# A rotating start for the projection's weights in their SBUF tile

## The chip, the cores and the metric

The kernel runs on one core of a Trainium2 chip. A core has TensorE (matmuls; the profile calls it PE, and its loading of weights PEld), VectorE (DVE), ScalarE (ACT), GpSimd (POOL) and SyncE (SP), which issues most of the DMAs. The metric is the time of one execution on the device in microseconds. The median of 3 runs before the change is 859.98 us (859.38 to 860.38).

## The reference

One layer of a decoder, for one sequence of 512 tokens and a model width of 2048, all in float32:

```python
h = rmsnorm(x, norm_g[l])
proj = h @ w_in[l]
(cv_a, cv_b, cv_gate, fq, fk, fv, f_logit, fox_gate,
 mq, mem_gate) = jnp.split(proj, SPLITS, axis=-1)
...
y = jnp.concatenate([y_conv, y_fox, y_mem], axis=-1)
x = x + y @ w_out[l]
return rmsnorm(x, final_g)
```

Behind the input projection stand three groups: a causal depthwise convolution of 31 taps with layer norm (512 channels), a forgetting attention of 8 heads of 128, and a cross attention of 4 heads into 256 memory tokens. Each is gated by a SiLU of its own part of the projection. The change is in the input projection, h @ w_in, which the kernel computes 128 output features at a time.

## The kernel before

**Two parts for each operand.** A float32 operand of a matmul is split into a high and a low part of the type float32r: ACT copies the raw tile into the high part (L93), DVE subtracts the high part from the raw tile and writes the low one (L94). A product is then three matmuls, high x high, high x low and low x high, which are summed in PSUM (mm3, L104 to L106; product, L739).

**The weights' tiles.** weights (L134) loads 2048 x 128 of w_in in two halves of 8 rows of 128, each with one DMA into a raw tile of 128 x 1024 elements (pool of 6), and calls operand (L120) on each. operand takes a tile "wb" of 2 x 1024 + 128 elements per partition from a pool of 3. The high part starts at element off of the tile and the low part 1024 elements later; the 128 spare elements are the room that off may use. off is in elements of 4 bytes. Three values are in use: PAIRED = 0, EVEN = 8 (32 bytes) and HEADS = 16 (64 bytes). Within a part, row k of 128 elements starts at 512 k bytes.

**The two forms of the projection.** The normalised input lies in SBUF for the whole projection, transposed and split, as tiles hh0 to hh7 and hl0 to hl7, two rows of 512 tokens in each.

- project (L304) computes 128 features for all 512 tokens: 16 rows x 3 matmuls with the weights stationary and 512 columns moving, with off=EVEN. It is called 22 times: 8 times for the convolution's two inputs, 4 times each for the memory queries, the memory gates and the convolution's gates, and twice for the first head's queries and keys.
- pair (L717) computes two times 128 features for all tokens with seven products of half the size in place of eight (Strassen's scheme): the raw weights are added and subtracted on DVE (less, L710), the sums of the input's quarters stand ready in the tiles s0, s1, s2. Each of its seven products calls operand with off=0 and runs 8 rows x 3 matmuls with 256 columns moving (L739). There are 15 pairs.

The other users of wb tiles are the memory's keys (L275, EVEN), the memory's values (L232) and the convolution's pointwise product (L593), both at 0, the output's plain part (L942, EVEN; there wb is the moving operand) and the output's heads (L983, HEADS; wb is the moving operand too).

**Addresses.** The pools put each of the three wb tiles 448 bytes past a multiple of 512, and all the moving tiles of the projection (hh, hl and the sums) 480 bytes past one. So project's weights start at 480, like its moving operand, and a pair's weights at 448, 32 bytes short of it, in terms of the place within 512 bytes.

**Order.** Every engine runs its instructions in order; the kernel's framework fixes that order ahead and puts in the semaphores. The weights' DMAs stand on SP's queue. With three wb tiles, one is read by TensorE while another is filled, and a third stands ready or is being filled.

Of the kernel before, what the change touches and what calls it, by code (L numbers as in the profile page):

```python
# [17 lines left out]
P = 128  # L18
S = 512
D = 2048  # L20
KT = D // P
# [26 lines left out]
def hybrid_layer_kernel(  # L48
# [20 lines left out]
    w_in, w_mem_kv, w_out, w_pw = w_in[0], w_mem_kv[0], w_out[0], w_conv_pw[0]  # L69
# [10 lines left out]
    def nm(s):  # L80
        uid[0] += 1
        return f"{s}_{uid[0]}"

    def pj(shape=(P, S)):
        return ps_pj.tile(list(shape), F32, tag="pj", name=nm("pj"))
# [4 lines left out]
    def split(hi, lo, src, scale=None):  # L90

        if scale is None:
            ins = nc.scalar.copy(hi, src)  # L93
            nc.vector.tensor_tensor(lo, src, hi.bitcast(F32), ALU.subtract)  # L94
        else:
            ins = nc.scalar.activation(hi, src, AF.Identity, scale=scale)
            nc.vector.scalar_tensor_tensor(
                lo, src, scale, hi.bitcast(F32), ALU.mult, ALU.subtract
            )
        return ins.ins  # L100

    def mm3(o, a, b, start, stop):
        (ah, al), (bh, bl) = a, b
        nc.tensor.matmul(o, ah, bh, start=start, stop=False)  # L104
        nc.tensor.matmul(o, ah, bl, start=False, stop=False)  # L105
        nc.tensor.matmul(o, al, bh, start=False, stop=stop)  # L106
# [3 lines left out]
    def background(n):  # L110
        for _ in range(min(n, len(bg))):
            bg.popleft()()

    def raw_tile(n, c):
        return wp.tile([P, n, c], F32, tag="raw", name=nm("raw"), bufs=6)

    PIECE = 8 * P
    PAIRED, EVEN, HEADS = 0, 8, 16

    def operand(src, out=None, off=0):  # L120

        if out is None:
            both = wp.tile([P, 2 * PIECE + P], F32R, tag="wb", name=nm("wb"), bufs=3)
            out = tuple(
                both[:, o : o + PIECE].rearrange("p (n c) -> p n c", c=src.shape[2])
                for o in (off, off + PIECE)
            )  # L130
        split(*out, src)
        return out

    def weights(src, n, c, raw=None, off=0):  # L134

        half = n // 2
        src = src.rearrange("(k p) f -> p k f", p=P)
        parts = []
        for j in range(2):
            rows = slice(j * half, (j + 1) * half)  # L140
            r = raw_tile(half, c) if raw is None else raw[:, rows, :]
            nc.sync.dma_start(out=r, in_=src[:, rows, :])
            parts.append(operand(r, off=off))
        return lambda k: tuple(t[:, k % half, :] for t in parts[k // half])


# [27 lines left out]
    with tc.tile_pool(name="start", bufs=1) as st:  # L174
# [49 lines left out]
        for q in range(4):  # L224
            qs = slice(q * QC, (q + 1) * QC)
            for t in range(MT):
                nc.sync.dma_start(out=mrow[t][:, qs], in_=mem[t * P : (t + 1) * P, qs])
            raw = None
            if q >= 2:
                raw = st.tile([P, D], F32, tag="rows", name=f"rv{q}", bufs=4)  # L230
                raw = raw.rearrange("p (k f) -> p k f", f=MW)
            wvs.append(weights(w_mem_kv[q * QC : (q + 1) * QC, MW : 2 * MW], 4, MW, raw))  # L232
            if q == 0:
                small, cwr = load_small()
                pt = at((P, KT))
                nc.tensor.transpose(pt, mgain, ident[:KT, :KT])
                nc.vector.tensor_copy(cols[:, :KT], pt)
            for k in range(4 * q, 4 * q + 4):
                pt = at((P, M))
                for t in range(MT):  # L240
                    nc.tensor.transpose(
                        pt[:, t * P : (t + 1) * P], mrow[t][:, k * P : (k + 1) * P], ident
                    )
                last = split(m_hi[k], m_lo[k], pt, scale=cols[:, k : k + 1])
            for kk in range(4):
                k = 4 * q + kk
                for t in range(MT):
                    sl = slice(t * P, (t + 1) * P)
                    mm3(os_[t], (m_hi[k][:, sl], m_lo[k][:, sl]), wvs[q](kk), k == 0, k == KT - 1)
# [24 lines left out]
        for h in range(NM):  # L274
            wk = weights(w_mem_kv[:, h * P : (h + 1) * P], KT, P, off=EVEN)  # L275
            load_x(h)
            norm_x(h)
            o = pj((P, M))
            for k in range(KT):
                mm3(o, wk(k), (m_hi[k], m_lo[k]), k == 0, k == KT - 1)  # L280
                if h == NM - 1:
                    x_column(k)
            if h == 0:
                pt = at((P, M))
                for t in range(MT):
                    nc.tensor.matmul(
                        pt[:, t * P : (t + 1) * P], ones, diag[:, t, :], start=True, stop=True
                    )
                nc.vector.tensor_copy(rbc, pt)
            kt = st.tile([P, M], F32, tag="kt", name=nm("kt"), bufs=1)  # L290
            nc.vector.tensor_tensor(kt, o, rbc, ALU.mult)
            split(mk[0][:, h, :], mk[1][:, h, :], kt)
# [10 lines left out]

    def project(f0, per=0):  # L304

        w = weights(w_in[:, f0 : f0 + P], KT, P, off=EVEN)
        o = pj()
        for k in range(KT):
            mm3(o, w(k), (h_hi[k], h_lo[k]), k == 0, k == KT - 1)
        background(per)  # L310
        return o
# [11 lines left out]
    with tc.tile_pool(name="conv", bufs=1, reuse_waits="tile") as cp:  # L323
# [19 lines left out]
        def conv_in(c):  # L343
            oa = project(C_A + c * P, 6)
            ob = project(C_B + c * P, 6)
            up = cp.tile([P, PAD + S], F32, tag="up", name=nm("up"), bufs=3)
            nc.gpsimd.memset(up[:, 0:PAD], 0.0)
            sg = cp.tile([P, S], F32, tag="sgb", name=nm("sgb"), bufs=2)
            nc.scalar.activation(sg, ob, AF.Sigmoid)
            nc.vector.tensor_tensor(up[:, PAD:], oa, sg, ALU.mult)  # L350
            taps_of(c, up)
# [242 lines left out]
        for k in range(NC):  # L594
            wh, wl = wpw(k)
# [98 lines left out]
    with tc.tile_pool(name="fox", bufs=1, reuse_waits="tile") as fx:  # L694
# [11 lines left out]
        def plus(o, p, q):  # L706
            nc.vector.tensor_tensor(o, p, q, ALU.add)

        def less(o, p, q):
            nc.vector.tensor_tensor(o, p, q, ALU.subtract)  # L710

        def kept(src, tag):
            t = fx.tile([P, M], F32, tag=tag, name=nm(tag), bufs=1)
            nc.scalar.copy(t, src)
            return t

        def pair(fa, fb):  # L717

            HK = KT // 2

            def load(f0, half):
                r = raw_tile(HK, P)
                rows = slice(half * HK * P, (half + 1) * HK * P)
                nc.sync.dma_start(
                    out=r, in_=w_in[rows, f0 : f0 + P].rearrange("(k p) f -> p k f", p=P)
                )
                return r

            def product(o, w, a, start=False):
                wh, wl = operand(w)
                for k in range(HK):
                    ah, al = (t[:, k % 2, :] for t in a[k // 2])
                    for i, (p, q) in enumerate(((wh, ah), (wh, al), (wl, ah))):
                        nc.tensor.matmul(  # L739
                            o, p[:, k, :], q, start=start and k == 0 and i == 0,  # L740
                            stop=k == HK - 1 and i == 2, skip_group_check=True,
                        )

            b11, b12, b22, b21 = load(fa, 0), load(fb, 0), load(fb, 1), load(fa, 1)
            x1, zo, x2 = (pj((P, M)) for _ in range(3))
            product(x1, b11, a11, start=True)
            yield
            p1 = kept(x1, "p1")
            less(b11, b12, b11)
            product(zo, b11, s1, start=True)  # L750
            p5 = kept(zo, "p5")
            less(b11, b22, b11)
            product(x2, b11, s2, start=True)
            plus(x2, x2, p1)
            u2 = kept(x2, "u2")
            product(x1, b21, a12)
            product(zo, b22, s4)
            less(b12, b22, b12)
            product(x2, b12, s3)
            col = fx.tile([P, S], F32, tag="col", name=nm("col"), bufs=2)  # L760
            plus(col[:, M:], x2, p5)
            plus(col[:, :M], zo, u2)
            less(b21, b21, b11)
            yield
            product(x2, b21, a22)
            yield (x1, x2), col
# [320 lines left out]
```

## Time and profile before

| what | us |
|---|---|
| median of the runs | 859.98 |
| the profiled execution's own time | 860.89 |
| its span, first to last instruction | 859.0 |
| TensorE busy | 844.9 |
| DVE busy | 703.7 |
| ACT busy | 435.6 |

The span divides into stages, read in windows of the trace: up to about 75 us the memory's keys and values and the transposes of the input; from there to 343 us the 22 calls of project (two of them for the first head), with the convolution's taps on DVE and the memory attention between them; from 343 to about 677 us the 15 pairs with the forgetting attention between them; then the output projection. A row of a group in the profile gives line, engine, operation, operands and count, then the busy time, the mean length of one instruction and the idle time ahead of it. In the chain of work that ended last, a row gives the start, the length and what ran, with a count where equal pieces are merged.

### The profile page before, as it was taken

Reading aid. Unit: us, or ns where it says so; the run is one execution under the profiler, and the core shown is the slowest. Engines: PE = TensorE matmul, PEld = TensorE weight load, DVE = VectorE, ACT = ScalarE, POOL = GpSimd, SP = SyncE. Lnnn points to the kernel's source line nnn. Section 1 sums busy time; section 2 is a strip of 40 time slices with the busy share of each in tenths; the row PEclk is TensorE's granted clock in tenths of the full one; section 3 lists DMA queues with packets and bytes.
Section 4 is the critical chain, followed back from the end, with each engine's and each line's share of the span. In section 5 each row is a group of like instructions: output and inputs, shape, how many; then the busy total and the mean of one; then the engine's idle time right before and its main releaser. Section 6 shows DMA issues by size and latency. Waiting matters only on the chain.

```text
span 859.0 us, 14010 instructions
## 1 busy us (share of the span) xinstructions
PE 844.9 (98%) x5562; PEld 773.0 (90%) x5562; DVE 703.7 (82%) x1051; ACT 435.6 (51%) x679; POOL 46.6 (5%) x76
## 2 busy tenths in 40 slices
PE   8999999999999999999999999999999999999996
PEld 6898888888888888999999999999999888998995
DVE  4586799999987998988787879888887986876964
ACT  4874332224445544666565656556564942443523
POOL 1011000000000002010101010101010000000001
PEclk8999999999999999999999999999999999999999
DMA  9973234332432443333434343433334627361415
GB/s 312 336 214 80 74 96 111 98 98 75 109 86 82 115 110 99 93 108 96 123 99 123 94 109 94 111 103 100 106 81 157 229 78 265 98 197 50 148 49 195
DMA packets 143264, 107.51 MB, mean 125 GB/s; under 512 B 3892, under 2 KB 126816, under 8 KB 142560
## 3 DMA queue, kind: packets, MB, share of 16 engines
q1 hardware_dynamic: 141696, 102.52, 41.4%
q0 software_dynamic: 1504, 4.11, 1.4%
q8 instruction: 43, 0.70, 0.3%
q14 instruction: 21, 0.17, 0.1%
HBM read 98.46 MB, written 8.14 MB: 124 GB/s over the span
## 4 chain that ended last, share of the span: by engine, by line
PE 95%; ACT 2%; issue 1%; DVE 1%; DMA 1%; SPq 0%; POOL 0%; ACTq 0%; POOLq 0%
PE pj L739 33%; PE pj L104 13%; PE pj L105 13%; PE pj L106 13%; PE pj L988 8%; PE at L104 3%; PE at L105 3%; PE at L106 3%; PE at L827 1%; DMA raw<-in_w_mem_kv_dram 1%; ACT wb L93 0%; PE pj L415 0%; PE pj L416 0%; PE pj L269 0%; PE at L789 0%
## 5 line engine op out<-in xcount | busy, mean ns | idle before, releaser
L93 ACT CAST wb<-raw 128x1024 fp32r<-128x1024 f32 x205 | 215.4, 1052 | 246.1 <-PE pj L106 73.2
L94 DVE TENSOR_TENSOR wb<-raw,wb 128x1024 fp32r<-128x1024 f32 x205 | 250.0, 1221 | 64.2 <-ACT wb L93 60.3
L739 PE MATMUL pj<-hh,wb 128*128 128x256 f32 x960 | 177.3, 280 | 0.0
L739 PEld LDWEIGHTS pj<-hh,wb 128*128 128x128 f32 x960 | 150.1, 188 | 0.0
L104 PE MATMUL pj<-hh,wb 128*128 128x512 f32 x352 | 137.3, 391 | 0.1
L105 PE MATMUL pj<-hl,wb 128*128 128x512 f32 x352 | 137.4, 391 | 0.0
L106 PE MATMUL pj<-hh,wb 128*128 128x512 f32 x352 | 137.2, 390 | 0.0
L739 PE MATMUL pj<-hl,wb 128*128 128x256 f32 x480 | 134.2, 280 | 0.0
L710 DVE TENSOR_TENSOR raw<-raw,raw 128x1024 f32<-128x1024 f32 x76 | 92.7, 1219 | 1.3 <-DMA raw<-in_w_out_dram 0.8
L739 PEld LDWEIGHTS pj<-hl,wb 128*128 128x128 f32 x480 | 90.2, 188 | 0.0
L336 DVE SCALAR_TENSOR_TENSOR acc<-up,cwt,acc 128x512 f32<-128x512 f32 x120 | 85.0, 742 | 0.4
L988 PE MATMUL pj<-wb,rh 128*128 128x256 f32 x672 | 80.2, 280 | 0.7 <-DVE res L914 0.7
L988 PEld LDWEIGHTS pj<-wb,rh 128*128 128x128 f32 x672 | 79.5, 188 | 1.4 <-DVE res L914 1.1
L104 PEld LDWEIGHTS pj<-hh,wb 128*128 128x128 f32 x352 | 66.1, 188 | 14.0 <-PE pj L269 0.3
L106 PEld LDWEIGHTS pj<-hh,wb 128*128 128x128 f32 x352 | 66.1, 188 | 13.7
L105 PEld LDWEIGHTS pj<-hl,wb 128*128 128x128 f32 x352 | 66.1, 188 | 13.5
L739 PE MATMUL pj<-s0h,wb 128*128 128x256 f32 x240 | 48.1, 288 | 0.0
L739 PE MATMUL pj<-s1h,wb 128*128 128x256 f32 x240 | 45.7, 280 | 0.0
L739 PE MATMUL pj<-s2h,wb 128*128 128x256 f32 x240 | 44.8, 279 | 0.0
L739 PEld LDWEIGHTS pj<-s0h,wb 128*128 128x128 f32 x240 | 38.5, 188 | 0.0
L739 PEld LDWEIGHTS pj<-s1h,wb 128*128 128x128 f32 x240 | 38.1, 188 | 0.3
L739 PEld LDWEIGHTS pj<-s2h,wb 128*128 128x128 f32 x240 | 37.8, 188 | 0.0
(292 smaller groups left out, 1439.9 us busy)
## 6 DMA issues: line engine op xcount, KB each, us to landing
raw<-in_w_in_dram SPq DMA_DIRECT2D x104, 512.0 KB, 3.9
raw<-in_w_out_dram SPq DMA_DIRECT2D x32, 512.0 KB, 4.6
raw<-in_w_mem_kv_dram SPq DMA_DIRECT2D x12, 512.0 KB, 8.5
xr<-in_x_dram SPq DMA_DIRECT2D x4, 1024.0 KB, 8.5
res<-in_x_dram SPq DMA_DIRECT2D x8, 512.0 KB, 7.2
out_dram<-res SPq DMA_DIRECT2D x16, 256.0 KB, 2.9
rs<-yd SPq DMA_DIRECT2D x15, 256.0 KB, 4.5
mr<-in_mem_dram SPq DMA_DIRECT2D x8, 256.0 KB, 7.5
```

The lines of the kernel that those rows point to most:

```text
L93: ins = nc.scalar.copy(hi, src)
L94: nc.vector.tensor_tensor(lo, src, hi.bitcast(F32), ALU.subtract)
L104: nc.tensor.matmul(o, ah, bh, start=start, stop=False)
L105: nc.tensor.matmul(o, ah, bl, start=False, stop=False)
L106: nc.tensor.matmul(o, al, bh, start=False, stop=stop)
L336: return lambda: nc.vector.scalar_tensor_tensor(a, up[:, j : j + S], cwt[:, c, j : j + 1], a, ALU.mult, ALU.add)
L710: nc.vector.tensor_tensor(o, p, q, ALU.subtract)
L739: nc.tensor.matmul(o, p[:, k, :], q, start=start and k == 0 and i == 0, stop=k == HK - 1 and i == 2, skip_group_check=True,)
L827: nc.tensor.transpose(tp[:, (i - j) * P : (i - j + 1) * P], pr[i][:, j * P : (j + 1) * P], ident)
L988: nc.tensor.matmul(o[:, m, :], p, q[:, k, :], start=start and k + m + i == 0, stop=k == HK - 1 and i == 2, skip_group_check=True,)
```

## The change

A list of 23 offsets is made once, in elements: 0 to 15, then 16, 32, 48, 64, 80, 96 and 112, which is 0 to 60 bytes in steps of 4 and 64 to 448 bytes in steps of 64. It is walked round and round. Each half of project's weights takes the next offset of the list, and so does each of the seven products of a pair. All other users of wb tiles keep their offsets. The high and the low part still stand 1024 elements apart, so both move by the same offset.

```diff
@@ -116,6 +116,7 @@
     PIECE = 8 * P
     PAIRED, EVEN, HEADS = 0, 8, 16
+    turns = itertools.cycle([*range(16), *range(16, P, 16)])
@@ -140,7 +141,7 @@
             nc.sync.dma_start(out=r, in_=src[:, rows, :])
-            parts.append(operand(r, off=off))
+            parts.append(operand(r, off=next(turns) if off is None else off))
@@ -303,7 +304,7 @@
     def project(f0, per=0):
-        w = weights(w_in[:, f0 : f0 + P], KT, P, off=EVEN)
+        w = weights(w_in[:, f0 : f0 + P], KT, P, off=None)
@@ -732,7 +733,7 @@
             def product(o, w, a, start=False):
-                wh, wl = operand(w)
+                wh, wl = operand(w, off=next(turns))
```

## The prediction, made before the change was run

> **What bounds the kernel now.** I read the page first: the span, the busy table and the chain of work that ended last.
>
> ```profile
> span 859.0 us, 14010 instructions
> ...
> PE 844.9 (98%) x5562; PEld 773.0 (90%) x5562; DVE 703.7 (82%) x1051; ACT 435.6 (51%) x679; POOL 46.6 (5%) x76
> ...
> PE 95%; ACT 2%; issue 1%; DVE 1%; DMA 1%; SPq 0%; POOL 0%; ACTq 0%; POOLq 0%
> ...
> L739 PE MATMUL pj<-hh,wb 128*128 128x256 f32 x960 | 177.3, 280 | 0.0
> ...
> L104 PE MATMUL pj<-hh,wb 128*128 128x512 f32 x352 | 137.3, 391 | 0.1
> ```
>
> The chain lies on TensorE for 95% of the span. The two matmul groups that take their weights from wb tiles in the input projection have no idle time ahead of them: 3 x 352 = 1056 matmuls of 512 columns (L104 to L106, the 22 calls of project), and 2520 of 256 columns (L739: 15 pairs x 7 products x 8 x 3). Next I asked for TensorE's waits, to see whether the weights ever come late.
>
> ```profile
> PE pj L104 <- ACT wb L93: 1.2, 1, 1.2
> ```
>
> That is the only wait of TensorE for a wb tile, 1.2 us in all. So in both groups the time is the number of matmuls times the pace, and the durations of the groups (391 and 280 ns) aren't that pace, since matmuls overlap. The pace is the distance from one start to the next, and I took it from the chain, whose rows give start, length and, when merged, a count.
>
> ```profile
> 98.04 0.23 PE pj L105
> ...
> 109.60 0.23 PE pj L105
> ```
>
> From 98.04 to 109.60 there are 51 matmuls of project in an unbroken row: 11.56 / 51 = 226.7 ns each.
>
> ```profile
> 395.78 13.66 PE pj L739 x117
> ...
> 421.84 13.90 PE pj L739 x118
> ...
> 788.74 14.02 PE pj L988 x120
> ```
>
> The pairs run at 13.66 / 117 = 116.8 ns in one stretch and 13.90 / 118 = 117.8 ns in another, 117.3 on the mean; the product at L988, at the same width, at 116.8.
>
> **Why the place of the weights can matter at all.** The change moves data by bytes, adds no instruction, no wait and no DMA. So its cost lies in what a matmul or a split costs at another address. I worked out the addresses that the kernel's own pools give. Each wb tile starts 448 bytes past a multiple of 512, and every moving tile of the projection (hh, hl, the three sums) 480 bytes past one; the rows k are 512 bytes apart. Call "gap" the start of the weights minus the start of the moving operand, modulo 512 bytes. In project (off=EVEN, 32 bytes) the gap is 0. In a pair (offset 0) it is -32, and at L988 (weights at 480, moving wb at 448 + 64) it is -32 too. The kernel also holds other gaps at the same widths. L415 and L416 multiply the same moving tiles, 512 columns, by wfs, which starts 320 bytes past a multiple of 512: gap -160.
>
> ```profile
> 90.33 0.23 PE pj L415
> ...
> 97.58 0.23 PE pj L416
> 97.82 0.23 PE pj L104
> ```
>
> From 90.33 to 97.82 the 32 matmuls take 7.49 us: 234.1 ns each, 7.4 ns more than project's matmuls directly behind them, with the same moving data. And for 256 columns at gap 0 there are the last output products, with both operands at 480:
>
> ```profile
> 830.28 0.12 PE at L105
> ...
> 831.24 0.12 PE pj L105
> 831.36 0.23 PE pj L104
> ```
>
> From 830.28 to 831.36 are nine matmuls: 1.08 / 9 = 120.0 ns, 2.7 more than the pairs' 117.3. So gap 0 is the quick one at 512 columns and the slow one at 256, and each half of the projection stands now at the quicker of the gaps that its width shows here.
>
> The Trainium skill, "TensorE: Matmul & The Clock Gate", Part 2, speaks against that: TensorE has two independent SBUF read ports, and loading the next weights takes no read bandwidth from the running matmul. By it the place of the weights would be worth nothing and the time would stay. The 7.4 ns above speak against it, so I keep it as a rival.
>
> **The change part by part.** The turns are taken in program order: first by the 44 halves of the 22 project calls, then by the 105 products. The list has 23 offsets: 0 to 60 bytes in steps of 4, and 64 to 448 in steps of 64. Every half and every product is 24 matmuls.
>
> *Project, 512 columns.* Offset 32 bytes, the present one, comes up in 2 of the 44 halves: nothing changes. Offsets that are multiples of 64 bytes come up in 14 (8 in the first round of 23, 6 in the other 21). They put the gap at -32, 32, 96, up to 352; the one such gap measured is that of wfs (-160 is 352). I price all 14 like it: 14 x 24 = 336 matmuls x 7.4 ns = 2.5 us. The remaining 28 halves, 672 matmuls, have gaps of -28 to 28 bytes, for which no row stands. Their ends are the two measured paces, 0 and +7.4 ns, so 0 to 5.0 us; gap 0 is near in bytes, but most of these starts are odd multiples of 4 bytes, which nothing here has, so I take the middle, 2.5 us. That the quick pace is not had at once speaks against the low end:
>
> ```profile
> 205.18 0.23 PE pj L106
> ...
> 206.80 0.23 PE pj L104
> ```
>
> Behind a group of transposes, 205.18 to 206.80, seven matmuls of project at gap 0 take 1.62 us, 231.4 ns each. The pace has to settle, and the change gives a new gap every 24 matmuls.
>
> *Pairs, 256 columns.* Offset 0 comes up in 5 of the 105 products: unchanged. Offset 32 bytes, gap 0, comes up in 5: 120 matmuls x 2.7 = 0.3 us. The other 95 products, 2280 matmuls, are unknown between 116.8 (the quicker stretch, -0.5 ns, -1.1 us) and 120.0 (+2.7 ns, 6.2 us). I take +1.1 ns, the middle: 2.5 us.
>
> *Splits.* ACT's cast (L93) and DVE's subtraction (L94) write, and L94 also reads, at the new starts. Here are both at 32 bytes (the stretch 100:300) and at 0 (340:660):
>
> ```profile
> L93 ACT CAST wb<-raw 128x1024 fp32r<-128x1024 f32 x33 | 34.6, 1048 | 78.1 <-PE pj L106 61.7 <-issue 15.9 <-ACT lu L432 0.5
> ```
>
> ```profile
> L94 DVE TENSOR_TENSOR wb<-raw,wb 128x1024 fp32r<-128x1024 f32 x33 | 40.2, 1218 | 2.2 <-ACT wb L93 1.7
> ```
>
> ```profile
> L93 ACT CAST wb<-raw 128x1024 fp32r<-128x1024 f32 x99 | 104.4, 1056 | 83.0 <-PE pj L739 61.3 <-issue 10.7 <-DVE raw L710 6.9
> ```
>
> ```profile
> L94 DVE TENSOR_TENSOR wb<-raw,wb 128x1024 fp32r<-128x1024 f32 x100 | 122.0, 1221 | 27.2 <-ACT wb L93 23.9 <-PE at L827 3.1
> ```
>
> 1048 against 1056 and 1218 against 1221 ns: no price for these two starts. I cost the splits at nothing. Their cover is the third wb tile: a split of 2.3 us (1.05 + 1.22) has 24 matmuls of another tile to run beside, 24 x 117.3 = 2.8 us in a pair and 5.4 us in project. If that cover went, each overrun would stand on the path.
>
> *The sum.* 2.5 + 2.5 + 0.3 + 2.5 = 7.8 us, all on TensorE's row and so on the path. The ends are 2.5 + 0 + 0.3 - 1.1 = 1.7 and 2.5 + 5.0 + 0.3 + 6.2 = 14.0. The profiled execution took 860.89 us (span 859.0 and 1.9 around it) and would take 868.7; the median of the runs is 859.98, 0.9 below, so 867.8, with 861.7 to 874.0 as this case's own range.
>
> **The rivals.**
>
> *The place doesn't matter, only the stream does.* The slow rows could be slow because they are short or use the same weights twice (L415 and L416 share wfs[:, k]), not because of their gap. Then any gap settles at the present pace: 860.0. For it: the settling above at one and the same gap, and two paces in the pairs at one gap. Against it: 32 matmuls at L415 and L416 never settle, and project stands at 226.7 as soon as they end. The skill's two ports are this case. The changes of tiles would then do what they say and cost nothing.
>
> *A better gap is found: faster.* Three gaps are known of 128 possible, and the kernel may be at a poor one everywhere. How much is there to find is seen where the clock is halved.
>
> ```profile
> 12.28:14.84 2.56, 2.56 (x7) 1.98 (x7) 1.40 (x2) 0.72 (x1) 0.00 (x0) 0.50 1.05 386
> ```
>
> ```profile
> 12.28 0.43 PE pj L104
> 12.70 0.43 PE pj L105
> 13.13 0.43 PE pj L104
> ```
>
> At a granted clock of 0.50 two matmuls of 512 columns start in 0.85 us, 425 ns each; at full clock that is 212.5, so 226.7 holds 14.2 ns that another gap could free. The 672 matmuls of unknown small gap would gain 9.5 us at most, and with the 2.5 of the multiples of 64 bytes lost the time is 853 (pairs left as they are). It decides from a mean pace of 223 ns in those 672: there gain and loss balance. Against it: neither known gap at this width is below 226.7.
>
> *DVE becomes the bound.* In 100:300 DVE has little idle time:
>
> ```profile
> 100.00:300.00 200.00, 200.00 (x922) 166.16 (x921) 183.94 (x282) 78.84 (x115) 2.86 (x6) 1.00 0.35 94
> ```
>
> 183.94 of 200 us. If starts off the multiples of 32 bytes made L94 slower, the idle 16 us would take it until its 33 instructions are 16.1 / 33 = 0.49 us longer on the mean, 1.7 us instead of 1.22. Were they doubled, the excess is 33 x 1.22 - 16.1 = 24 us, on top of the above: about 892. Nothing in the trace points there.
>
> **How the numbers follow.** A gap-dependent pace, slower: 0.73, at 867.8. No dependence: 0.13, at 860.0. A better gap: 0.08, at 853. DVE or an odd start that costs far more: 0.06, above 874. A measurement of this kernel can tell about 0.2%, 1.7 us, from no change; the first case's low end is at that bound, so its chance counts as slower, with the last one's: slower 0.79, same 0.13, faster 0.08. The range 860.5 to 874.0 holds the first case and part of the second, and leaves out the third and the last.
>
> **What would show it.** In the profile of the changed kernel, the instruction counts of every group stay. In the chain, project's rows fall into pieces of 24 matmuls with a pace of their own: 226.7 ns in the halves at 32 bytes, near 234 at multiples of 64. The sums in the stretch of project grow by about 5 us, in that of the pairs by about 3. L93 and L94 keep 1.05 and 1.22 us, TensorE's wait for wb stays near 1.2 us, and L988 keeps 116.8 ns. I am wrong if every half has one pace, if an odd start is below 226.7 ns, or if L94 grows.

## The result, and the profile after

The change makes the kernel slower by about 1%: 869.17 us (median of 3 runs, 868.56 to 869.39) against 859.98 before, a ratio of 1.0106 with a 95% interval of 1.0083 to 1.0129. The forecast was 867.8, in a range of 860.5 to 874.0.

The page of the changed kernel, with the same parts as above (its lines behind the new one have numbers higher by one, so the pairs' matmuls are L740):

```profile
span 866.8 us, 14010 instructions
...
PE 853.0 (98%) x5562; PEld 776.4 (90%) x5562; DVE 704.7 (81%) x1051; ACT 434.7 (50%) x679; POOL 45.2 (5%) x76
...
PE 96%; issue 1%; DVE 1%; DMA 1%; ACT 1%; SPq 0%; POOL 0%; POOLq 0%; ACTq 0%
...
L93 ACT CAST wb<-raw 128x1024 fp32r<-128x1024 f32 x205 | 215.1, 1051 | 252.3 <-PE pj L106 71.7
L94 DVE TENSOR_TENSOR wb<-raw,wb 128x1024 fp32r<-128x1024 f32 x205 | 250.1, 1221 | 67.6 <-ACT wb L93 63.6
L740 PE MATMUL pj<-hh,wb 128*128 128x256 f32 x960 | 180.1, 282 | 0.0
...
L105 PE MATMUL pj<-hl,wb 128*128 128x512 f32 x352 | 139.0, 395 | 0.0
```

All counts are the same. The splits (L93, L94) keep 1.05 and 1.22 us, and the matmuls of the projection still have no idle time ahead. What has grown is TensorE's busy time, by 8.1 us, inside an unbroken stream: the pace has changed.

From the starts of the matmuls in the two traces I summed the time from each start to the next, by part. Project's 1056 matmuls took 241.1 us before and 245.9 after (+4.8), the pairs' 2520 took 299.5 and 303.6 (+4.1), and the 672 of the output's heads, which the change doesn't touch, 79.9 in both. That is 8.9 us; the span grew by 7.8 only, because the changed kernel's profiled execution came to its first matmul of project 1.0 us earlier (65.8 against 66.8 us). The medians are 9.2 apart. In eight traces of kernels that are the same up to there (before, and seven of the experiments) that start lies between 65.3 and 66.9 us, so the 1.0 us can be chance; how much of it the medians hold isn't known.

Two halves of project in the chain of the changed kernel (start, length, what), the first at gap 0, the second at gap 28:

```profile
120.97 0.23 PE pj L106
...
124.14 0.23 PE pj L105
```

```profile
158.41 0.23 PE pj L104
...
163.58 0.24 PE pj L105
```

From 120.97 to 124.14 there are 14 matmuls, 226.4 ns each; from 158.41 to 163.58 there are 22, 235.0 ns each. And two products of the pairs, cut out of the chain by narrow windows, at gap 8 and at gap 0:

```profile
610.99 2.08 PE pj L740 x18
```

```profile
678.11 2.40 PE pj L740 x20
```

2.08 / 18 = 115.6 ns and 2.40 / 20 = 120.0 ns. Read in this way for every half and product, the changed kernel is a table of pace against gap:

| gap, bytes | 512 columns, ns | 256 columns, ns |
|---|---|---|
| -32 | 233.2 | 117.1 |
| -16 | 226.6, 228.4 | 118.9 |
| -8 | 233.3 | 117.9 |
| -4 | 226.7, 233.3 | 119.9 |
| 0 | 226.7, 229.1 | 119.9 |
| 8 | 230.7 | 115.9 |
| 16 | 228.2, 233.2 | 118.4 |
| 24 | 231.0 | 121.0 |
| 28 | 235.0 | 116.6, 116.6, 120.0, 133.3 |
| 32 | 233.1 | 118.2 to 118.4, 133.3 |
| 96 | 234.0 | 119.0 |
| 224 | 233.4 | 116.8 |
| 288 | 233.1 | 118.3 |
| 352 (-160) | 234.3 | 118.2 |

At 512 columns each is the mean of two halves, or both where they lie more than 1 ns apart (gap 352 has one half, and the row of wfs from before lies near it, at 234.1). At 256 columns each is the mean of four or five products. At about half of the 23 gaps these agree within 1 ns, those at gap 8 between 115.4 and 116.1; at the others some lie 1 to 4 ns off the rest, and at gaps 28 and 32, which stand product by product, one of four ran at 133.3. So the pace does hang on the gap, but along no simple curve, and not on the gap alone: gap -4 had two paces in its two halves. At 512 columns nothing is quicker than the 226.4 ns read above at gap 0.

### The profile page after: what moved, and what is told of

It reads as the page before. It is cut to its first block, busy times and chain, and to the rows that moved or that the text cites. A ratio compares the mean times of both kernels' runs of the same rounds, so it can differ in the third digit from the quotient of the medians.

```text
span 866.8 us, 14010 instructions
## 1 busy us (share of the span) xinstructions
PE 853.0 (98%) x5562; PEld 776.4 (90%) x5562; DVE 704.7 (81%) x1051; ACT 434.7 (50%) x679; POOL 45.2 (5%) x76
## 4 chain that ended last, share of the span: by engine, by line
PE 96%; issue 1%; DVE 1%; DMA 1%; ACT 1%; SPq 0%; POOL 0%; POOLq 0%; ACTq 0%
PE pj L740 34%; PE pj L104 13%; PE pj L105 13%; PE pj L106 13%; PE pj L989 8%; PE at L104 3%; PE at L105 3%; PE at L106 3%; PE at L828 1%; DMA raw<-in_w_mem_kv_dram 1%; PE pj L416 0%; PE pj L417 0%; PE pj L270 0%; PE at L790 0%; PE at L390 0%
## 5 line engine op out<-in xcount | busy, mean ns | idle before, releaser
L93 ACT CAST wb<-raw 128x1024 fp32r<-128x1024 f32 x205 | 215.1, 1051 | 252.3 <-PE pj L106 71.7
L94 DVE TENSOR_TENSOR wb<-raw,wb 128x1024 fp32r<-128x1024 f32 x205 | 250.1, 1221 | 67.6 <-ACT wb L93 63.6
L740 PE MATMUL pj<-hh,wb 128*128 128x256 f32 x960 | 180.1, 282 | 0.0
L740 PEld LDWEIGHTS pj<-hh,wb 128*128 128x128 f32 x960 | 151.0, 188 | 0.0
L104 PE MATMUL pj<-hh,wb 128*128 128x512 f32 x352 | 138.8, 395 | 0.1
L106 PE MATMUL pj<-hh,wb 128*128 128x512 f32 x352 | 138.6, 394 | 0.0
L740 PE MATMUL pj<-hl,wb 128*128 128x256 f32 x480 | 135.1, 281 | 0.0
L740 PEld LDWEIGHTS pj<-hl,wb 128*128 128x128 f32 x480 | 90.4, 188 | 0.0
L989 PE MATMUL pj<-wb,rh 128*128 128x256 f32 x672 | 80.2, 279 | 0.7 <-DVE sst L1043 0.4
L740 PE MATMUL pj<-s0h,wb 128*128 128x256 f32 x240 | 48.6, 289 | 0.0
L740 PE MATMUL pj<-s1h,wb 128*128 128x256 f32 x240 | 46.3, 282 | 0.0
L740 PE MATMUL pj<-s2h,wb 128*128 128x256 f32 x240 | 45.3, 281 | 0.0
L740 PEld LDWEIGHTS pj<-s0h,wb 128*128 128x128 f32 x240 | 38.7, 189 | 0.0
L740 PEld LDWEIGHTS pj<-s1h,wb 128*128 128x128 f32 x240 | 38.4, 188 | 0.3
L740 PEld LDWEIGHTS pj<-s2h,wb 128*128 128x128 f32 x240 | 37.9, 188 | 0.0
```

Of the source, the lines that this page charges most:

```text
L740: nc.tensor.matmul(o, p[:, k, :], q, start=start and k == 0 and i == 0, stop=k == HK - 1 and i == 2, skip_group_check=True,)
L989: nc.tensor.matmul(o[:, m, :], p, q[:, k, :], start=start and k + m + i == 0, stop=k == HK - 1 and i == 2, skip_group_check=True,)
```

## The experiments

My theory was that a matmul's pace in these streams is set by the gap between the start of its weights and that of its moving tile. The rivals: that changing the place every 24 matmuls disturbs the stream; that the weights' own address counts, not the distance; and that the place doesn't matter. Medians below stand beside runs of the kernel before on the same chip.

**One part at a time.** Only project takes turns, then only the pairs:

```diff
-                wh, wl = operand(w, off=next(turns))
+                wh, wl = operand(w)
```

> Only the project halves take turns; the pairs stay at offset 0 (gap -32). If a matmul's pace is set by the gap of its own weights to its moving tile, project takes what it took in the changed kernel, 245.9 us against 241.1 before, and the pairs 299.5 as before: +4.8 us, 864.8. If the changes disturb the stream as a whole, both parts grow. If the place doesn't matter: 860.

```diff
-        w = weights(w_in[:, f0 : f0 + P], KT, P, off=None)
+        w = weights(w_in[:, f0 : f0 + P], KT, P, off=EVEN)
```

> Only the products of the pairs take turns; project stays at gap 0. By the gap: the pairs take 303.6 us instead of 299.5 and project 241.1 as before: +4.1 us, 864.1 (and with the other half 860.0 + 4.8 + 4.1 = 868.9, near the changed kernel's 869.2). If the two halves are not separate, the two runs don't add up.

Measured: 865.03 us (ratio 1.0058, 1.0043 to 1.0073) and 864.11 (1.0045, 1.003 to 1.006), against 860.47 before. In the first, project took 245.9 us and the pairs 299.7; in the second 241.1 and 303.2. The parts are separate: +4.6 and +3.6 us, 8.2 of the 9.2 together, with intervals of about 1.3 us on each.

**A constant place.** Project at offset 0 throughout, nothing takes turns:

```diff
-        w = weights(w_in[:, f0 : f0 + P], KT, P, off=EVEN)
+        w = weights(w_in[:, f0 : f0 + P], KT, P)
```

> Project stays at one offset, 0, so at gap -32, and nothing changes from matmul to matmul. By the gap: 233.1 ns a matmul as in the changed kernel's halves at offset 0, so (233.1 - 226.7) x 1056 = +6.8 us, 866.8, more than all 23 offsets in turn cost (+4.8). If it is the change every 24 matmuls that costs, a constant offset costs nothing: 860.

Measured: 866.54 us (1.0073, 1.0056 to 1.009). The chain has one pace all along; these are its rows across four halves:

```profile
103.63 0.23 PE pj L106
...
124.63 0.23 PE pj L106
```

21.00 us for 90 matmuls: 233.3 ns. No turn is taken, and project takes 247.4 us, 1.5 more than with the turns. The rival of the disturbance falls, since a constant place costs as much as that place did in turn (233.3 ns here, 233.2 there). So does "the place doesn't matter": these streams are as long as those before.

**Distance or address.** All moving tiles lie 32 bytes lower, behind a small tile put in ahead of them, and project's weights too; the pairs' weights stay:

```diff
+    shift = ctx.enter_context(tc.tile_pool(name="shift", bufs=1, side="right"))
+    shift.tile([P, EVEN], F32, name="shift")
...
-        w = weights(w_in[:, f0 : f0 + P], KT, P, off=EVEN)
+        w = weights(w_in[:, f0 : f0 + P], KT, P)
```

(The output's offsets were moved along, EVEN to 0 and HEADS to 8.)

> All moving tiles of the projection lie 32 bytes lower (448 in place of 480, modulo 512) and project's weights 32 bytes lower too, so project keeps gap 0 at a new address; the pairs' weights stay where they were, so their gap goes from -32 to 0. The output's two parts keep their gaps. If the gap counts: project 226.7 ns as before, the pairs 120.0 in place of 117.2, +7.1 us, 867.1. If the weights' own address counts: project 233.3 as with weights at 448, +6.3 us, and the pairs unchanged, 866.3. The totals lie close; the two paces tell the cases apart.

Measured: 866.07 us against 859.80 (1.0069, 1.0054 to 1.0085). Project's rows, and a window of the pairs:

```profile
98.04 0.23 PE pj L104
...
109.60 0.23 PE pj L104
```

```profile
344.89 6.12 PE pj L741 x51
```

11.56 / 51 = 226.7 ns with the weights at the address that gave 233.3 in the run before, and 6.12 / 51 = 120.0 ns with the pairs' weights where they had always been. Summed, project took 241.1 us as before and the pairs 305.7, +6.2. The moving tiles' own address doesn't explain it either: with them at 480 as before, gap 0 gave the pairs the same 120.0 ns in the changed kernel. As far as this one shift of 32 bytes shows, the distance counts, not the address.

**A map of the rest.** The changed kernel tries 23 of the 128 gaps that whole elements allow. Here the pairs take the other 105 and project 44 of them:

```diff
-    turns = itertools.cycle([*range(16), *range(16, P, 16)])
+    others = [o for o in range(17, P) if o % 16]
+    halves_ = itertools.cycle([others[i * 105 // 44] for i in range(44)])
+    turns = itertools.cycle(others)
...
-            parts.append(operand(r, off=next(turns) if off is None else off))
+            parts.append(operand(r, off=next(halves_) if off is None else off))
```

> A look only: each of the 105 products takes one of the 105 offsets between 68 and 508 bytes that the change left out, each half of project one of 44 of them. By the gap every 24 matmuls have a pace of their own, within 115.6 to 123.0 ns for 256 columns and 226.7 to 235.0 for 512, smooth in the gap as from 8 to 32 bytes; time about 868 to 870. If only gaps near 0 matter, all 105 have one pace, near 119. A pace below 115.6 would show a better place.

Measured: 868.60 us in one run. At 512 columns none of the 44 gaps ran below 226.6 ns, and the slowest at 237.7 (gap 420). At 256 columns most stood between 116.5 and 121, but a few well below:

```profile
565.77 2.27 PE pj L742 x20
```

```profile
574.41 2.27 PE pj L742 x20
```

Gaps 320 and 332: 2.27 / 20 = 113.5 ns, 3.7 below the pairs before. Gap 88 was another. So the bounds that were expected from the table were passed on both sides, at both widths, and the pace isn't smooth in the gap.

The table of the changed kernel and the map together show one order, though: the pace repeats after 256 bytes. Here is gap 264 in the map:

```profile
523.79 2.31 PE pj L742 x20
```

2.31 / 20 = 115.5 ns, the pace of gap 8; its neighbours 260 and 268 ran at 118.0 and 116.7, as 4 and 12 had at 118.2 and 117.0. In the table above -32 and 224, and 32 and 288, are couples of this kind. At 512 columns gaps 28 and 284 both ran at 235.0 and gaps 212 and 468 both at 236.7. Of the 23 couples of gaps 256 bytes apart that both runs together hold at that width, 17 agree within 0.3 ns; of 22 couples 128 bytes apart, 7 do.

**Holding the quick gaps.** First 320 for the pairs and the heads, then 332 for the pairs alone (offsets 88 and 91, and 56 for the heads):

```diff
-    PAIRED, EVEN, HEADS = 0, 8, 16
+    PAIRED, EVEN, HEADS = 88, 8, 56
...
-                wh, wl = operand(w)
+                wh, wl = operand(w, off=PAIRED)
```

> Project as before at gap 0; the pairs and the output's heads at gap 320 (-192), where the one product of the map that had it ran at 113.5 ns. If the pace is fixed by the gap: (117.2 - 113.5) x 2520 + (117.1 - 113.5) x 672 = 9.3 + 2.4 = 11.7 us less, 848.3. If that product was quick by chance (the state of the stream at its start), the pace falls back to 117 to 120 and the time is 860 to 868.

> The pairs alone at gap 332 (-180), 113.35 ns in its one product of the map; the heads stay at gap -32. By the gap: (117.2 - 113.4) x 2520 = 9.6 us less, 850.4, and the heads at 117.1 as before. By chance of the start: 860 to 868.

Measured: 855.86 us (0.9955, 0.9943 to 0.9967) and 857.59 (0.9972, 0.9961 to 0.9983). The kernel before took 859.80 beside them, so both are faster, and by less than half of what was expected (3.9 and 2.2 us of 11.7 and 9.6). Here the theory, as I had put it, falls. In the run at gap 332, two windows of the pairs:

```profile
427.93 2.15 PE pj L739 x19
```

```profile
438.66 13.68 PE pj L739 x114
452.34 0.22 PE at L789 x2
452.56 0.76 PE at L827 x7
453.32 2.75 PE pj L739 x24
```

2.15 / 19 = 113.2 ns in one. In the other, 13.68 / 114 = 120.0 ns, at one gap, over several products without a change; then come nine transposes (L789, L827), and behind them the stream goes at 2.75 / 24 = 114.6 ns, its slow first steps included. At gap 320 the two paces are 113.3 and 117.8. The slow one begins behind other matmuls or transposes that were put into the stream, holds through product after product, and ends behind the next such break; from the third head on it lies in the same products of every head. So a gap can have two steady paces, and they change behind breaks in the stream. Gap -32 has them too, 116.7 and 117.8, which are the two stretches of pairs that the prediction averaged. With the order of 256 bytes the map had held the slow paces as well: gap 64, 256 bytes from 320, ran at 117.8 there, and gap 76, 256 bytes from 332, at 120.0.

**One gap with one pace, and a mixture.** Gap 8 was quick in all five of its products. In the mixture, gap 332 stays where it had kept 113.3:

```diff
+            offs = iter([91, 91] + [PAIRED if fa >= F_G else 91] * 5)
...
-                wh, wl = operand(w)
+                wh, wl = operand(w, off=next(offs))
```

with PAIRED, EVEN, HEADS = 10, 8, 6; the other run has off=PAIRED throughout.

> The pairs and the output's heads at gap 8, which the changed kernel showed at 115.4 to 116.1 ns in all five of its products, without a second pace. If gap 8 has one pace whatever the stream's state: (117.2 - 115.6) x 2520 + (117.1 - 115.6) x 672 = 4.0 + 1.0 = 5.0 us less, 855.0. If it has a second pace as gaps 320 and 332 have (117.8, 120.0) once it is held through a whole pair: 857 to 862.

> Gap 332 where the run with it alone kept 113.3 ns (the query and key pairs, and the first two products of a gate and value pair), gap 8 in the five products of a gate and value pair that ran at 120.0; the heads at gap 8. If a product's pace is set by its gap and by the state in which the stream enters: about 9 of 14 products at 113.7 and 5 of 14 at 115.6, mean 114.5, (117.2 - 114.5) x 2520 + 1.0 = 7.8 us less, 852.2. If the slow state lies in those five products and not in the gap, they run at 117 or more: 854 to 857.

Measured: 859.14 us (0.9987, 0.9978 to 0.9996) and 856.98 (0.9958, 0.9945 to 0.997), against 860.23. The pairs came near to what was expected: at gap 8 every product ran at 115.5 to 117.0, mean 115.9, and the mixture's mean was 115.0; summed, they took 3.0 and 5.4 us less, of 4.0 and 6.8. In the mixture the third product of the query and key pairs, at gap 332, ran, from the third head on, at 113.4 ns for one head and at 120.0 for the next, in turn, so the slow pace doesn't belong to a product. The heads did not do what was expected. Their row at gap 8:

```profile
722.89 14.41 PE pj L988 x120
```

14.41 / 120 = 120.1 ns, 3.3 above the row before. That took back 1.6 us in both runs. In the heads wb is the moving operand and not the stationary one, and the pairs' table isn't theirs; the runs don't show which property of the two streams makes the difference.

**The heads' own map**, with the pairs as in the mixture but for two wavering products, now at gap 8 as well:

```diff
+        spots = iter([0, 2, 4, 12, 14, 18, 20, 24, 28, 32, 36, 40, 44, 48, 53, 58, 62, 66, 70, 75, 80, 84, 88, 96, 104, 112, 117, 120])
...
-            wh, wl = operand(w, off=HEADS)
+            wh, wl = operand(w, off=next(spots))
```

> A look: the 28 products of the output's heads, where wb is the moving operand, each take an offset of their own (48 matmuls each does not apply here: 24 per product), so 28 gaps. The mixed run's heads went to 120.0 at gap 8, where the pairs have 115.6. If the pace of the heads is fixed by a gap of their own, each product has a pace between 113.3 and 123 and gap 8's 120.0 is one of them; if the heads' pace is always 117 or more, no place frees anything there. The two products of each query and key pair that wavered between 113.4 and 120.0 are at gap 8 now: 115.6 each.

Measured: 856.03 us in one run. The 28 products ran between 113.3 and 123.4 ns: gap 332 at 120.0, gaps 368, 400 and 496 at 113.3 to 113.6. Gaps 8 and 332 have another pace there than the quick one in the pairs.

**The best version that I ran**: project at gap 0, the pairs at 332 and 8, the heads at 368.

```diff
-    PAIRED, EVEN, HEADS = 0, 8, 16
+    PAIRED, EVEN, HEADS = 10, 8, 44
...
+            offs = iter([91, 91] + [PAIRED] * 5 if fa >= F_G else [91, PAIRED, PAIRED, 91, 91, 91, 91])
```

> Project at gap 0; the pairs at gaps 332 and 8 as in the run before, which had 114.9 ns on the mean: (117.2 - 114.9) x 2520 = 5.8 us less. The heads all at gap 368, where one of their products ran at 113.3. If that pace holds: (117.1 - 113.3) x 672 = 2.6 us less again, 851.6; if it falls back to a second pace of 118 to 120: 854 to 856.

Measured: 855.00 us (853.76 to 855.59) against 860.16, a ratio of 0.9936 with an interval of 0.9922 to 0.9949. Two stretches of its pairs, which took 13.66 and 13.90 us before:

```profile
394.92 13.49 PE pj L740 x117
...
420.73 13.41 PE pj L740 x118
```

The pairs' mean is 114.9 ns, 5.5 us less in all. The heads, held at gap 368, fell back to 116.7 and 118.5 ns and gained nothing: 80.2 us against 79.9.

## Why the prediction was right, and where its sizes were off

**The pace of an unbroken stream sets the time: right.** No wait appeared (TensorE waited 1.0 us for a wb tile, 1.2 before), what the pace cost came through in the time (8.9 us in the parts; 7.8 in the span and 1.0 of earlier start), and the splits cost nothing at any of the 23 starts. The rival in which DVE becomes the bound is out.

**Project.** The halves at multiples of 64 bytes were sized at 2.5 us and measured 2.1. They ran at 233.1 to 234.3 ns where wfs had 234.1, and the halves that stood there before weren't all at 226.7: with the slow first steps behind breaks, the unbroken steps of project were 227.2 on the mean. The halves at small gaps, taken at the middle between nothing and +7.4 ns, measured 2.7 against the 2.5 forecast. That the middle came out is luck, since it was taken for want of a row, and it was right only as a mean: single gaps lie all the way from 226.7 to 235.0, and gaps -16, -12, -4 and 16 gave 226.6 to 228.2 in one half and 228.4 to 233.3 in the other. Project as a whole: 5.0 forecast, 4.8 measured.

**Pairs.** Gap 0 was priced at 0.3 us and cost 0.3. The other 95 products are the term that was mis-sized: +1.1 ns on each matmul and 2.5 us forecast, 1.6 ns and 3.7 us measured. Both ends that I had taken from the rows, 116.8 and 120.0, were passed: gap 8 ran at 115.9, gap 24 at 121.0, two products at 133.3. Two measured points don't bound a quantity whose order isn't known.

**From the span to the median.** The profiled execution was forecast at 868.7 and took 868.56. That agreement is luck and better than the terms: the parts grew by 8.9 us where the sum had 7.8, and the early start of project hid 1.0 of it. The median moved by 9.2.

**The rivals.** "The place doesn't matter" had it right that the stream has a state of its own, and wrong that any gap would settle at the present pace: gap -32 in project stayed at 233.3 ns for the whole stage. "A better gap is found" was wrong about project, where none of 67 gaps is below 226.6 ns, and the 14 ns that I read out of the half clock were not found at any of them. It was right about the pairs, where I had not looked for it: 113.3 ns exists, though it can't be held by the gap alone.

**The two independent read ports** of the Trainium skill ("TensorE: Matmul & The Clock Gate", Part 2) do not make the place of weights and moving data free: the run at a constant gap of -32 shows a price of 6.6 ns in 226.7 at 512 columns, and the one with the moved tiles shows that it goes by the distance between the two.

What stays open is the mechanism. The runs show that the distance, modulo 256 bytes by the two tables, and the state of the stream go with the pace; none of them shows why, or whether the load of the weights and the read of the moving tile meet anywhere in the chip. Nor was it tried which instruction throws a stream from one of its paces into the other.

## What to carry to other kernels

Where TensorE runs without idle time, measure its pace from start to start, not the length of a matmul, and compare it between streams of one shape: a few nanoseconds that differ may be the place of the operands, and are worth their number times some thousand matmuls. A kernel that walks through many offsets in one run is slow by itself but measures them all at once, and such a map must be checked by holding the place found, since a quick sample of 24 matmuls may not last. A table made for one stream isn't valid for another: gap 8, quick in the pairs, was slow in the heads.

## What was not expected of the hardware

- At one and the same gap a stream of 256-column matmuls has two steady paces, 113.3 and 120.0 ns at gap 332, 113.3 and 117.8 at gap 320, 116.7 and 117.8 at gap -32, and keeps the one it has until other instructions come between.
- The pace repeats after 256 bytes of distance: 235.0 ns at gaps 28 and 284, 115.6 and 115.5 at gaps 8 and 264.
- One element, 4 bytes, changes the pace by up to several nanoseconds: in the map gap 84 ran at 119.5, gap 88 settled at 113.3 and gap 92 ran at 118.1, and gaps 340, 344 and 348, each 256 bytes further, at 120.3, 114.1 and 118.1.
- A start off every multiple of 8 bytes costs nothing by itself, neither for the splits (1.05 and 1.22 us as before) nor for the matmuls: gap 12 ran at 117.0 ns for 256 columns, as gap -32 did, and one half at gap -4 at 226.7 for 512, as gap 0 did.
